# A hybrid decoder layer on one core: the squares of the first norm summed by TensorE, rotary angles moved ahead, the condition row built on chip, and low halves of weights moved from GpSimd to VectorE

## The chip, the core and the metric

The kernel runs on one core of a Trainium2 chip. The core has a matrix engine (TensorE, PE in the profile; its weight loads are PEld), a vector engine (VectorE, DVE), an activation engine (ScalarE, ACT), a general engine (GpSimd, POOL), and a queue engine (SyncE, SP) that issues nearly all transfers. Each engine works through its own queue in order and waits on semaphores. The metric is the device time of one execution in microseconds, as the median of several runs.

## What is computed

One layer (2048 tokens, width 1024): an adaptive norm, one input projection whose columns feed a sliding-window attention and a state-space mixer, an output projection with a gated residual, then the same norm with other weights, a gated feed-forward part of width 2816, another residual and a last norm. What matters for the change:

```python
def rmsnorm(x, w):
    y = x * lax.rsqrt(jnp.mean(x * x, axis=-1, keepdims=True) + EPS)
    return y * w
...
mod = jax.nn.silu(c) @ w_ada[layer] + b_ada[layer]         # c has one row of 1024, mod 6 x 1024
shift1, scale1, gate1, shift2, scale2, gate2 = jnp.split(mod, N_MOD, axis=-1)
h = modulate(rmsnorm(x, norm1_w[layer]), shift1, scale1)   # h * (1 + scale) + shift
x = x + gate1 * hybrid_mixer(h, positions, ...)            # proj = h @ w_in; q and k get rotary angles
```

The rotary step multiplies halves of q and k by the cosine and sine of position times a frequency.

## The kernel before, in words

All matrices are fp32. A large product is made of three products of halves: an operand is split into a high half (a rounded copy, made by ScalarE) and a low half (the rest, made by a subtraction), and `mm3` (L269 to 272) adds high-high, high-low and low-high. So each weight tile costs a load into `raw`, a high half (L262) and a low half (L263) in `weight` (L254 to 267). Before the change L263 runs on GpSimd by default, on VectorE where the caller says so: the first halves of the convolution's weights (L468) and the later output projections (L811). Weights that come again are written back split, and loaded so by the later blocks.

The 2048 tokens are four blocks of 512. Activations lie with the width on the partitions: eight tiles `xT[b, d]` of 128 x 512 for a block. For each block the kernel normalizes x (`norm1`), projects queries, keys and values, convolved channels and gates, then runs attention and the mixer as side work, then the output projection.

`norm1` (L340 to 352) has four steps. It loads the eight tiles, squares them on ScalarE and adds the squares up on GpSimd (`square_into`, L274 to 280); it sums over the partitions with small PE products against ones and takes the reciprocal root by integer tricks on VectorE (`rstd`, L282 to 286, `root_of`, `rsqrt`); it spreads the root over the partitions with four diagonals and one PE product (`spread`, L309 to 315); then it loads x again and makes the modulated halves (`modulated`, L317 to 323). Its later steps are tied to counts of PE's main steps.

The modulation `mod` has 48 columns of 128 values. Column i is a row-wise reduction on VectorE of a tile of `wada` times the silu of c, which lies in `csil` as one row of 1024 on all partitions; before the change `csil` is loaded spread, 512 KB, and its silu taken on the chip (L145 to 151). Four of the first columns come by PE products instead (`ada_products`, L169). The other 32 columns, not needed by the first norm, are made by `ada_later` (L184 to 196): two loads of 256 KB into a ring of two buffers `aw` and two reductions at L195. Their loads are queued behind the opening's last weight load, their reductions behind the opening's last VectorE instruction, by `tc.issue_after`, which puts what is traced in its block, on the named instruction's own engine, behind that instruction in issue order.

Order: in `opening` (L1241) the order of PE, VectorE, SP and ScalarE is written out by hand; it loads x and the first modulation rows, squares, norms, modulates, and runs the first projection as pairs of weight tiles arrive (`pair_ready`, `first_columns`). Its last step is the first quarter of the rotary tables (`rope_tables`, L209 to 231). After it only PE's order is written by hand; the other engines' order comes from a scheduler that works with modelled times and takes what was traced first among what is ready, and it may pull work traced later into gaps of the opening. Rotary steps read cosine and sine at L372 and 373 and are finished at L375, by GpSimd for most blocks. `out_proj` (L805) squares its results for the second norm.

Of the kernel before, what the change touches and what calls it, by code (L numbers as in the profile page):

```python
# [43 lines left out]
def hymba_layer(ctx, tc, xT, crow, pos, wada, wadk, vecs, rows, wq, wkv, wz, wx, wo, wgu, wd, outT):  # L44
# [62 lines left out]
    row = const([P, 32], "row")  # L107
    nc.sync.dma_start(row, rows.broadcast_to([P, 32]))
    posi = const([P, S // P], "posi", I32, pool=ip)
    nc.sync.dma_start(posi, pos)  # L110

# [8 lines left out]
    nc.gpsimd.memset(ones, 1.0)  # L120
    upper = const([P, P], "upper")
# [17 lines left out]
    invf = const([P, HALF], "invf", pool=ip)  # L139
    freqs = np.float32(ROPE_THETA) ** (-np.arange(HALF, dtype=np.float32) / np.float32(HALF))  # L140
    for j in range(HALF):
        nc.gpsimd.memset(invf[:, j:j + 1], float(freqs[j]))
# [3 lines left out]
    nc.sync.dma_start(csil, crow.broadcast_to([P, D]))  # L146

    def silu_c(i):
        cs, th = csil[:, i * T:(i + 1) * T], common.m2()
        nc.scalar.activation(th, cs, AF.Tanh, scale=0.5)  # L150
        nc.vector.scalar_tensor_tensor(cs, th, 1.0, cs, ALU.add, ALU.mult)
# [32 lines left out]
    def ada_later(i):  # L184
        halves = [slice(0, T), slice(T, D)]
        ws = [big("aw", 2, pool=ip) for _ in halves]
        with tc.issue_after(last_fetched.ins):
            for w, hs in zip(ws, halves):
                nc.sync.dma_start(w, wada[i, :, hs])
        for _ in range(2):  # L190
            yield
        m, pt = mod[:, i:i + 1], small([P, 1], "part", 2, pool=ip)
        with tc.issue_after(first_done.ins):
            for w, hs, src, dst in zip(ws, halves, (b_ada[:, i:i + 1], pt), (pt, m)):
                nc.vector.tensor_tensor_reduce(w, w, csil[:, hs], 0.5, src, ALU.mult, ALU.add, dst)  # L195
        yield
# [12 lines left out]
    def rope_tables(lo, hi):  # L209
# [10 lines left out]
        for dst, turn in ((sin, 0.0), (cos, 0.25)):  # L220
            k, r = work(), work()
            nc.vector.tensor_scalar(k, ang, 1.0 / (2 * math.pi), turn, ALU.mult, ALU.add)
            nc.vector.tensor_scalar(k, k, ROUND, None, ALU.add)
            nc.vector.tensor_scalar(k, k, ROUND, turn, ALU.subtract, ALU.subtract)
            nc.vector.scalar_tensor_tensor(r, k, -TWO_PI_1, ang, ALU.mult, ALU.add)
            nc.vector.scalar_tensor_tensor(r, k, -TWO_PI_2, r, ALU.mult, ALU.add)
            nc.vector.scalar_tensor_tensor(r, k, -TWO_PI_3, r, ALU.mult, ALU.add)
            rope_tables.last = nc.vector.tensor_scalar(r, r, PI_IN, -PI_IN, ALU.min, ALU.max)
            angles.append((dst, r))
        for dst, r in angles:  # L230
            nc.scalar.activation(dst[:, lo:hi, :].rearrange("p t j -> p (t j)"), r, AF.Sin)
# [22 lines left out]
    def weight(src, n, key, store, eng=nc.gpsimd, fresh=False):  # L254
# [8 lines left out]
        eng.tensor_tensor(lo, raw[:, :n], hi.bitcast(F32), ALU.subtract)  # L263
# [24 lines left out]
    def root_of(st, n, eng=nc.vector):  # L288
        ms = small([P, NT], "ms", 1, pool=cst)[:, 0:n]
        nc.vector.tensor_scalar(ms, st[:, 0:2 * n].rearrange("p (t k) -> p t k", k=2)[:, :, 0], 1.0 / D, EPS,  # L290
                                ALU.mult, ALU.add)
# [170 lines left out]
    def convolved(b, h):  # L462
        for c in range(8):
            ps = dense()
            for half in range(2):
                if half:
                    yield
                whi, wlo = weight(wx[c, half], T, ("x", c, half), b == 0, nc.gpsimd if half else nc.vector)  # L468
# [336 lines left out]
    def out_proj(b, y_of, mix, bank_of, acc, norm=None, each=lambda c: None):  # L805
        for c in range(KT):
            ps = bank_of(c)
            for half in range(2):
                if half:
                    yield  # L810
                whi, wlo = weight(wo[c, half], T, ("o", c, half), b == 0, nc.gpsimd if b < 2 else nc.vector, b > 1)  # L811
# [8 lines left out]
            square_into(acc, x, c == 0)  # L820
# [420 lines left out]
    def opening():  # L1241
        acc, h, x0 = tmp(), [], []
# [35 lines left out]
        def pair_ready(kp, raws):  # L1278
# [17 lines left out]
            nc.gpsimd.tensor_tensor(ws[2][1], raws[2], ws[2][0].bitcast(F32), ALU.subtract)  # L1296
            first_ws.append(ws)

        rows0, rows1 = rows_of(0, common.m4), rows_of(1, common.m4)
        raws = [fetched(0)]  # L1300
# [5 lines left out]
        rows4, rows5 = rows_of(4, extra.m4), rows_of(5, extra.m4)  # L1306
        reduced(8, rows0[0])
        st, line = side_bank(1), side_bank(0)
        for t in range(NT):
            nc.tensor.matmul(st[:, 2 * t:2 * t + 2], acc[:, t * P:(t + 1) * P], ones[:, 0:2], start=True, stop=True)  # L1310
        reduced(0, rows0[1])
        scale_of(0)
        bc = spread(root_of(st, NT), bc=side_bank(1))
# [24 lines left out]
        rope_tables(0, NT)  # L1338
        return h, main, fetched.last

    first_ws = []
    with tc.manual_schedule(engines={mybir.EngineType.PE, mybir.EngineType.DVE, mybir.EngineType.SP,
                                     mybir.EngineType.Activation}):
        h, main, last_fetched = opening()
        first_done = rope_tables.last
# [69 lines left out]
    with tc.manual_schedule(engines={mybir.EngineType.PE}):  # L1415
        with tc.issue_after(first_done.ins):
# [5 lines left out]
            pending.append([14, lambda: rope_tables(NT, S // P)])  # L1422
# [184 lines left out]
def _layout(x, c, positions, w_ada, b_ada, norm1_w, w_in, conv_w, conv_b, dt_bias, a_log, d_skip, attn_sinks,  # L1607
# [4 lines left out]
    out["crow"] = a(c.reshape(1, D))  # L1612
# [52 lines left out]
```

## Time and profile before

| | us |
|---|---|
| median of three runs | 2269.98 (2266.66 to 2273.71) |
| the profiled execution | 2267.25 |
| its span, first to last instruction | 2265.4 |
| PE busy | 2166.4 |
| VectorE busy | 1681.7 |
| ScalarE busy | 1008.4 |
| GpSimd busy | 700.2 |

The profile's views are: a page with busy times; busy times of each engine in chosen stretches, with the clock that TensorE's throttle granted (1.00 is full speed), the share of time in which the 16 DMA engines were busy, and GB/s; groups of equal instructions by line (busy time, mean ns of one, idle time before them and who ended it); waits (who waited for whom: total, times, longest); and the instructions in order of time (start, duration, engine, line, operation, what ended the idle time before). The lines L are those of the kernel before. An fp32 product of PE is shown as two instructions. The matmuls overlap: their durations are longer than the distance from one to the next.

### The profile page before, as it was taken

The page shows a single profiled execution, that of the slowest core. Times are in us where ns is not written, and L with a number is a line of the kernel's source. Part 1 is how long each engine was busy: PE and PEld are TensorE (multiplying, and loading weights), DVE is VectorE, ACT ScalarE, POOL GpSimd, SP SyncE. Part 2 cuts the span into 40 slices and gives each one's busy share as a digit, 9 for nine tenths or more (in the row PEclk, how much of TensorE's full clock was granted, in tenths as well). Part 3 has the DMA queues.
Part 4 walks back from the last instruction along what each step waited for, and adds up shares of the span by engine and source line. Part 5 has one row for each costly group of instructions (what it writes and reads, how often), then busy time and mean ns, then how long its engine had stood idle before and what let it go on. Part 6 is the DMA issues. An engine that isn't in the chain of part 4 may idle for free. (4 is left out here: it accounts for less than half of the span.)

```text
span 2265.4 us, 33515 instructions
## 1 busy us (share of the span) xinstructions
PE 2166.4 (96%) x11072; PEld 1801.9 (80%) x11072; DVE 1681.7 (74%) x3147; ACT 1008.4 (45%) x2113; POOL 700.2 (31%) x806
## 2 busy tenths in 40 slices
PE   6888988999999999999999999998999999999998
PEld 5778788888978888888888877777888888788887
DVE  8987976774549887788787768987777775776565
ACT  4564543665345655433344444532333333554342
POOL 2655533545123311144342222222333331110021
PEclk9988999999999999999999999999999999999998
DMA  8898988788879523234335579977333335777553
GB/s 296 293 318 298 319 259 258 252 265 271 291 244 339 198 91 110 94 117 126 94 103 182 190 259 310 328 225 227 125 98 105 98 91 197 270 261 268 171 168 100
DMA packets 289325, 470.45 MB, mean 208 GB/s; under 512 B 27392, under 2 KB 97024, under 8 KB 289152
## 3 DMA queue, kind: packets, MB, share of 16 engines
q1 hardware_dynamic: 288576, 467.80, 62.4%
q8 instruction: 87, 1.43, 0.3%
q14 instruction: 86, 0.70, 0.1%
q10 hardware_dynamic: 576, 0.52, 0.1%
HBM read 335.50 MB, written 132.71 MB: 207 GB/s over the span
## 5 line engine op out<-in xcount | busy, mean ns | idle before, releaser
L1090 PE MATMUL d<-a,w 128*128 128x512 f32 x1716 | 405.6, 396 | 7.0 <-DVE a L1062 3.9
L1090 PEld LDWEIGHTS d<-a,w 128*128 128x128 f32 x1716 | 321.6, 188 | 87.8 <-DVE a L1062 5.7
L951 PE MATMUL d<-b,w 128*128 128x512 f32 x924 | 366.0, 400 | 4.4 <-ACT t L975 4.4
L953 PE MATMUL d<-b,w 128*128 128x512 f32 x924 | 366.8, 398 | 1.9 <-DVE w L843 1.9
L952 PE MATMUL d<-b,w 128*128 128x512 f32 x924 | 367.5, 398 | 0.0
L280 POOL TENSOR_TENSOR acc<-acc,t 128x512 f32<-128x512 f32 x70 | 106.2, 1518 | 404.4 <-ACT t L279 389.8
L951 PEld LDWEIGHTS d<-b,w 128*128 128x128 f32 x924 | 174.5, 189 | 44.6 <-ACT t L975 5.5
L842 ACT ACTIVATE w<-s 128x512 fp32r<-128x512 f32 x176 | 110.8, 632 | 221.5 <-PE d L953 174.3
L953 PEld LDWEIGHTS d<-b,w 128*128 128x128 f32 x924 | 174.5, 189 | 42.5 <-DVE w L843 2.6
L952 PEld LDWEIGHTS d<-b,w 128*128 128x128 f32 x924 | 174.9, 189 | 38.6
L270 PE MATMUL d<-w,hl 128*128 128x256 f32 (+1 forms) x592 | 175.8, 297 | 6.9 <-ACT hl L321 4.5
L272 PE MATMUL d<-w,hl 128*128 128x256 f32 (+1 forms) x592 | 171.4, 289 | 1.8 <-DVE hl L322 1.8
L271 PE MATMUL d<-w,hl 128*128 128x256 f32 (+1 forms) x592 | 171.1, 289 | 0.0
L270 PE MATMUL d<-hl,w 128*128 128x512 f32 x352 | 146.3, 416 | 4.3 <-ACT w L262 2.2
L843 DVE TENSOR_TENSOR w<-s,w 128x512 fp32r<-128x512 f32 x176 | 143.2, 815 | 8.6 <-ACT w L842 7.3
L1086 DVE TENSOR_TENSOR w<-raw,w 128x512 fp32r<-128x512 f32 x156 | 107.2, 696 | 53.6 <-ACT w L1085 53.4
L272 PE MATMUL d<-hl,w 128*128 128x512 f32 x352 | 140.5, 399 | 1.4 <-DVE w L263 0.7
L842 ACT ACTIVATE w<-raw 128x512 fp32r<-128x512 f32 x132 | 82.9, 630 | 130.4 <-PE d L953 59.1
L271 PE MATMUL d<-hl,w 128*128 128x512 f32 x352 | 139.6, 397 | 0.0
L1085 ACT ACTIVATE w<-raw 128x512 fp32r<-128x512 f32 x156 | 90.7, 588 | 102.7 <-PE d L1090 67.5
L1062 DVE TENSOR_TENSOR a<-a 128x512 fp32r<-128x512 f32 x154 | 107.5, 720 | 37.3 <-ACT a L1061 37.0
L1005 POOL TENSOR_TENSOR t<-t 128x512 f32<-128x512 f32 x44 | 75.3, 1712 | 180.5 <-DVE t L1004 124.1
(414 smaller groups left out, 5017.7 us busy)
## 6 DMA issues: line engine op xcount, KB each, us to landing
raw<-in_wgu_dram SPq DMA_DIRECT2D x176, 256.0 KB, 2.9
w<-w_x SPq DMA_DIRECT2D x48, 512.0 KB, 5.1
act_t<-t SPq DMA_DIRECT2D x88, 256.0 KB, 3.3
a<-act_t SPq DMA_DIRECT2D x88, 256.0 KB, 4.8
t<-in_xT_dram SPq DMA_DIRECT2D x80, 256.0 KB, 4.2
act_b<-t SPq DMA_DIRECT2D x66, 256.0 KB, 2.2
a<-act_b SPq DMA_DIRECT2D x66, 256.0 KB, 5.0
aw<-in_wada_dram SPq DMA_DIRECT2D x64, 256.0 KB, 4.5
```

The source lines that it names most:

```text
L270: nc.tensor.matmul(out, ahi, bhi, start=first, stop=False)
L271: nc.tensor.matmul(out, ahi, blo, start=False, stop=False)
L272: mm3.last = nc.tensor.matmul(out, alo, bhi, start=False, stop=last)
L280: eng.tensor_tensor(acc, acc, sq, ALU.add)
L842: nc.scalar.activation(hi, x, AF.Copy)
L843: eng.tensor_tensor(lo, x, hi.bitcast(F32), ALU.subtract)
L951: nc.tensor.matmul(out, ahi, bhi, start=first and k == 0, stop=False, skip_group_check=True)
L952: nc.tensor.matmul(out, ahi, blo, start=False, stop=False, skip_group_check=True)
L953: mm3.last = nc.tensor.matmul(out, alo, bhi, start=False, stop=k == 3, skip_group_check=True)
L1062: nc.vector.tensor_tensor(lo, raw, hi.bitcast(F32), ALU.subtract)
L1086: nc.vector.tensor_tensor(w[1], raw, w[0].bitcast(F32), ALU.subtract)
L1090: mm3.last = nc.tensor.matmul(ps, w[x][:, ws], act[k][y][:, ts], start=new and k == 0 and x + y == 0, stop=k == KP - 1 and x == 1, skip_gr ...
```

## The change

- The condition row: the load of `csil` goes. The silu of c is taken on the eight columns that `vec` holds already, and two PE products of ones with diagonals spread it; ScalarE copies it to `csil`.
- The opening's squares: ScalarE squares as before, into a tile of its own each time, and PE adds up with 32 small products into one bank, in place of VectorE's additions and four products. The root now stands ahead of the second reduction.
- The angles of the first rotary quarter are made ahead of the squares, the Sin activations right behind them; both were the opening's last step. The frequencies' memsets stand earlier in GpSimd's queue; the load of the row of constants stands behind the first four modulation rows.
- `norm1` loads x with the tokens on the partitions (`xtok`, again eight tiles of 256 KB); ScalarE's square adds up along the row (`accum_out`), so the additions on GpSimd and the products of `rstd` go.
- `weight` and the third weight of `pair_ready` make every low half on VectorE. `out_proj` adds squares on VectorE for blocks 0 and 1, on GpSimd for 2 and 3 as before.
- `ada_later` names PE's last traced product in `issue_after` for the loads, and nothing for the reductions.

```diff
-    nc.sync.dma_start(csil, crow.broadcast_to([P, D]))
+    def silu_rows():
+        for i in range(2):
+            dg, bk = tmp(), side_bank(i)
+            for j in range(4):
+                nc.vector.tensor_scalar(dg[:, j * P:(j + 1) * P], ident, ccol[:, 4 * i + j:4 * i + j + 1], 0.0,
+                                        ALU.mult, ALU.add)
+            nc.tensor.matmul(bk, ones, dg, start=True, stop=True)
+            nc.scalar.copy(csil[:, i * T:(i + 1) * T], bk)
...
-        with tc.issue_after(last_fetched.ins):
+        with tc.issue_after(mm3.last.ins):
             for w, hs in zip(ws, halves):
                 nc.sync.dma_start(w, wada[i, :, hs])
...
-        with tc.issue_after(first_done.ins):
-            for w, hs, src, dst in zip(ws, halves, (b_ada[:, i:i + 1], pt), (pt, m)):
-                nc.vector.tensor_tensor_reduce(w, w, csil[:, hs], 0.5, src, ALU.mult, ALU.add, dst)
+        for w, hs, src, dst in zip(ws, halves, (b_ada[:, i:i + 1], pt), (pt, m)):
+            nc.vector.tensor_tensor_reduce(w, w, csil[:, hs], 0.5, src, ALU.mult, ALU.add, dst)
...
-        eng.tensor_tensor(lo, raw[:, :n], hi.bitcast(F32), ALU.subtract)
+        nc.vector.tensor_tensor(lo, raw[:, :n], hi.bitcast(F32), ALU.subtract)
...
     def norm1(b, h):
-        acc = sums()
-        for d in range(KT):
-            square_into(acc, load_x(b, d), d == 0)
-        yield
-        y = rstd(acc)
+        ss = small([P, 2, NT], "ssq", 1, pool=ip)
+        for t in range(NT):
+            for i in range(2):
+                x = tmp()
+                nc.sync.dma_start(x, xtok[b * NT + t, i])
+                nc.scalar.activation(x, x, AF.Square, accum_out=ss[:, i, t:t + 1])
+        yield
+        ms = small([P, NT], "ms", 1, pool=cst)
+        nc.vector.tensor_tensor(ms, ss[:, 0, :], ss[:, 1, :], ALU.add)
+        y = root_of_sum(ms, NT)
...
-            square_into(acc, x, c == 0)
+            square_into(acc, x, c == 0, nc.vector if b < 2 else nc.gpsimd)
...
     def opening():
+        silu_columns()
+        silu_rows()
         nc.vector.tensor_copy(posf, posi)
-        silu_columns()
-        for i in range(2):
-            silu_c(i)
+        angles = rope_angles(0, NT)
+        st = side_bank(2)
         for d in range(KT):
-            square_into(acc, x0[d], d == 0, nc.vector)
+            sq = tmp()
+            nc.scalar.activation(sq, x0[d], AF.Square)
+            for t in range(NT):
+                nc.tensor.matmul(st[:, 2 * t:2 * t + 2], sq[:, t * P:(t + 1) * P], ones[:, 0:2], start=d == 0 and t == 0,
+                                 stop=d == KT - 1 and t == NT - 1, skip_group_check=True)
+        rope_tables(angles)
...
-            nc.gpsimd.tensor_tensor(ws[2][1], raws[2], ws[2][0].bitcast(F32), ALU.subtract)
+            last = nc.vector.tensor_tensor(ws[2][1], raws[2], ws[2][0].bitcast(F32), ALU.subtract)
...
         reduced(8, rows0[0])
-        st, line = side_bank(1), side_bank(0)
-        for t in range(NT):
-            nc.tensor.matmul(st[:, 2 * t:2 * t + 2], acc[:, t * P:(t + 1) * P], ones[:, 0:2], start=True, stop=True)
+        bc = spread(root_of(st, NT), bc=side_bank(1))
         reduced(0, rows0[1])
         scale_of(0)
-        bc = spread(root_of(st, NT), bc=side_bank(1))
```

More of the change, by code (lines that the diff above doesn't have):

```diff
@@ L106, in hymba_layer @@
     nc.sync.dma_start(vec, vecs)
-    row = const([P, 32], "row")
-    nc.sync.dma_start(row, rows.broadcast_to([P, 32]))
     posi = const([P, S // P], "posi", I32, pool=ip)
     nc.sync.dma_start(posi, pos)
+    row = const([P, 32], "row")
     b_ada, n1w, n2w, fw_ = vec[:, 0:48], vec[:, 48:56], vec[:, 56:64], vec[:, 64:72]
@@ L120, in hymba_layer @@
     nc.gpsimd.memset(ones, 1.0)
+    invf = const([P, HALF], "invf", pool=ip)
+    freqs = np.float32(ROPE_THETA) ** (-np.arange(HALF, dtype=np.float32) / np.float32(HALF))
+    for j in range(HALF):
+        nc.gpsimd.memset(invf[:, j:j + 1], float(freqs[j]))
     upper = const([P, P], "upper")
@@ L227, in rope_tables @@
             nc.vector.scalar_tensor_tensor(r, k, -TWO_PI_3, r, ALU.mult, ALU.add)
-            rope_tables.last = nc.vector.tensor_scalar(r, r, PI_IN, -PI_IN, ALU.min, ALU.max)
-            angles.append((dst, r))
+            nc.vector.tensor_scalar(r, r, PI_IN, -PI_IN, ALU.min, ALU.max)
+            angles.append((dst[:, lo:hi, :].rearrange("p t j -> p (t j)"), r))
+        return angles
+    def rope_tables(angles):
         for dst, r in angles:
-            nc.scalar.activation(dst[:, lo:hi, :].rearrange("p t j -> p (t j)"), r, AF.Sin)
+            nc.scalar.activation(dst, r, AF.Sin)
     def rsqrt(y, ms, n, eng=nc.vector, tag="rsq", pool=cst):
@@ L252, in hymba_layer, with weight @@
     split_d = {}
[L254 removed]
+    def weight(src, n, key, store, fresh=False):
         two = wt.tile([P, 2, 528], F32R, name="w", tag="w", bufs=SPLIT)
@@ L467, in convolved @@
                     yield
-                whi, wlo = weight(wx[c, half], T, ("x", c, half), b == 0, nc.gpsimd if half else nc.vector)
+                whi, wlo = weight(wx[c, half], T, ("x", c, half), b == 0)
                 for i in range(4):
@@ L810, in out_proj @@
                     yield
-                whi, wlo = weight(wo[c, half], T, ("o", c, half), b == 0, nc.gpsimd if b < 2 else nc.vector, b > 1)
+                whi, wlo = weight(wo[c, half], T, ("o", c, half), b == 0, b > 1)
                 for i in range(4):
@@ L1241, in opening @@
     def opening():
-        acc, h, x0 = tmp(), [], []
+        h, x0 = [], []
         for d in range(KT):
@@ L1295, in pair_ready @@
                 nc.vector.scalar_tensor_tensor(h[d][1], xs[i], sh1[:, d:d + 1], h[d][0].bitcast(F32), ALU.add, ALU.subtract)
-            nc.gpsimd.tensor_tensor(ws[2][1], raws[2], ws[2][0].bitcast(F32), ALU.subtract)
+            last = nc.vector.tensor_tensor(ws[2][1], raws[2], ws[2][0].bitcast(F32), ALU.subtract)
+            pair_done[0] = last
             first_ws.append(ws)
         rows0, rows1 = rows_of(0, common.m4), rows_of(1, common.m4)
+        nc.sync.dma_start(row, rows.broadcast_to([P, 32]))
         raws = [fetched(0)]
@@ L1344, in hymba_layer @@
         h, main, last_fetched = opening()
-        first_done = rope_tables.last
+        first_done = pair_done[0]
     nc.scalar.activation(neg_a, a_log, AF.Exp)
```

27 lines of the change are left out of this document (10 added, 17 removed).

## The prediction

> **What bounds the kernel now.** I read the page first, then the busy times by stage, then TensorE's waits, then the opening in order of time, and last the groups on VectorE and GpSimd.
>
> ```profile
> PE 2166.4 (96%) x11072; PEld 1801.9 (80%) x11072; DVE 1681.7 (74%) x3147; ACT 1008.4 (45%) x2113; POOL 700.2 (31%) x806
> 0.00:30.00 30.00, 11.36 (x26) 3.58 (x26) 22.12 (x49) 10.68 (x18) 6.20 (x50) 1.00 0.93 346
> 30.00:60.00 30.00, 29.98 (x248) 29.55 (x248) 27.62 (x43) 14.27 (x23) 10.46 (x7) 1.00 0.74 246
> 60.00:130.00 70.00, 58.78 (x282) 46.97 (x282) 68.85 (x177) 40.01 (x90) 38.84 (x42) 0.95 0.89 311
> 130.00:240.00 110.00, 95.56 (x673) 88.68 (x672) 83.82 (x212) 58.07 (x138) 65.61 (x77) 0.89 0.91 309
> 240.00:380.00 140.00, 122.96 (x800) 109.90 (x798) 105.85 (x244) 61.31 (x145) 54.83 (x92) 0.96 0.82 266
> 380.00:800.00 420.00, 409.46 (x2506) 352.33 (x2505) 289.08 (x707) 227.93 (x566) 156.64 (x216) 1.00 0.78 263
> ```
>
> TensorE (PE) is busy 96% of the span, so at most 99 us of idle time can be won. The rows by stage (PE busy first, then weight loads, VectorE, ScalarE, GpSimd, granted clock, DMA share) say where it is: 18.6 us before 30, 11.2 in 60 to 130, 14.4 in 130 to 240, 17.0 in 240 to 380, 10.5 in the 420 us after that. From 800 on the change alters nothing, as the late output projections keep VectorE for the low halves and GpSimd for the squares. So the case is decided in the first 380 us. In 60 to 130 VectorE is busy 68.85 of 70 us: it is the bound there. In 130 to 240 it isn't (83.82 of 110), the DMA share is 0.91, and the granted clock is 0.89: PE waits in pieces long enough to lose its clock.
>
> ```profile
> PE d L270 <- ACT w L262: 2.2, 1, 2.2
> PE d L270 <- DVE s L373: 1.1, 1, 1.1
> PE d L270 <- DVE dt L451: 1.0, 1, 1.0
> PE am L271 <- POOL w L263: 1.0, 1, 1.0
> PE d L272 <- POOL w L263: 0.6, 1, 0.6
> PE d L270 <- ACT hl L321: 4.5, 2, 2.4
> PE am L270 <- ACT hl L321: 3.5, 1, 3.5
> ```
>
> These are PE's waits: five in 60 to 130 that the change touches (5.9 us together), then those for the normalized tiles of block 1 (8.0 us).
>
> **The opening, step by step.**
>
> ```profile
> 2.73 0.21 ACT L155 ACTIVATE t<-vec 128x8 f32<-128x8 f32 x1 [0.65 <-DMA vec<-in_vecs_dram]
> 8.57 4.50 ACT L279 ACTIVATE t<-m 128x512 f32<-128x512 f32 x7
> 14.83 1.84 PE L1310 MATMUL at<-ones,t 128*128 128x2 f32 x8 [14.83 <-DVE t L280]
> 17.09 0.15 DVE L290 TENSOR_SCALAR ms<-at 128x4 f32<-128x4 f32 x1
> 19.45 0.88 DVE L312 TENSOR_SCALAR t<-ident,rstd 128x128 f32<-128x128 f32 x4
> 20.24 1.28 DVE L1267 CUSTOM_DVE_ANT_0 m<-m,csil,vec 128x1024 f32<-128x1024 f32 x1
> 20.47 2.04 PE L314 MATMUL at<-t,ones 128*128 128x512 f32 x2 [3.80 <-DVE t L312]
> 22.45 7.68 PE L171 MATMUL am<-hl,vec 128*1 128x512 f32 x16
> 22.72 1.40 DVE L1288 SCALAR_TENSOR_TENSOR t<-m,scl,at 128x512 f32<-128x512 f32 x2
> 30.07 0.38 PE L270 MATMUL d<-w,hl 128*128 128x256 f32 x1
> L285 PE MATMUL d<-ones,acc 128*128 128x2 f32 x40 | 4.8, 241 | 0.0
> 75.62 0.58 ACT L475 COPY cin<-d 128x512 f32<-128x512 f32 x1 [1.81 <-PE d L272]
> ```
>
> Now the condition row no longer comes by a transfer of 512 KB but from the 8 columns. The tanh stays at 2.73; eight diagonals at 0.88 us for four (L312) are done near 5.1; two full-width fp32 products at 2.04 us each (L314) end near 8.3; each is copied by ScalarE at the price of L475, 0.58 us. So the row is whole near 8.9. The squares, behind those copies in ScalarE's order, then run from about 8.9 to 14.0 (eight at 4.50 us for seven), 0.9 us later than now.
>
> VectorE's seven additions go, and PE sums instead: 8 squares by 4 groups of tokens, 32 products, each two instructions, 64 instructions. This price has two ends in the trace. Right after idleness eight of them took 1.84 us (L1310), 0.23 each; in the flow 40 took 4.8 us (L285), 0.12 each. So 7.7 us warm, 14.7 us cold, both slower than ScalarE delivers (0.64 us a square against 0.96 or 1.84): PE sets the pace from the first square's end at 9.5, and the sums end at 17.2 or 24.2 instead of 16.67. PE has run the two products from about 4.2 on and pauses for only a microsecond, so I choose near the warm end: a quarter at the cold price, 16 by 0.23 and 48 by 0.12, 9.4 us, done near 18.9. The Trainium skill (TensorE: Matmul & The Clock Gate, Part 1) says that a busy window of about 3.4 us lifts the clock and an idle one drops it; the two rows above, 0.23 after idleness and 0.12 in the flow, agree. By the rule the time would be the forecast's, by the first row alone about 5 us more; whether such tiny products count as busy, no run here shows.
>
> From the sums the old chain follows: root and diagonals 17.09 to 20.33, 3.3 us; then, since the root now stands ahead of the second reduction, three reductions of 1.21 us and two small steps, 3.8 us, instead of two. The first L1288 thus starts at 18.9 + 0.2 + 3.3 + 3.8 = 26.2 instead of 22.72. Its block is 5.0 us long now; the next fence says what that loses and gains.
>
> ```profile
> 24.64 0.75 DVE L1295 SCALAR_TENSOR_TENSOR hl<-t,mod,hl 128x512 fp32r<-128x512 f32 x1
> 25.49 1.68 POOL L1296 TENSOR_TENSOR w<-raw,w 128x528 fp32r<-128x528 f32 x1 [20.34 <-ACT w L1292]
> 25.91 1.81 DVE L1295 SCALAR_TENSOR_TENSOR hl<-t,mod,hl 128x512 fp32r<-128x512 f32 x1
> L1296 POOL TENSOR_TENSOR w<-raw,w 128x528 fp32r<-128x528 f32 x4 | 6.7, 1675 | 42.7 <-ACT w L1292 42.7
> L263 POOL TENSOR_TENSOR w<-raw,w 128x512 fp32r<-128x512 f32 x24 | 33.5, 1399 | 28.3 <-ACT w L262 21.0 <-DMA raw<-in_wq_dram 3.6 <-DMA aw<-in_wada_dram 3.4
> L263 POOL TENSOR_TENSOR w<-raw,w 128x528 fp32r<-128x528 f32 x12 | 17.3, 1445 | 15.3 <-ACT w L262 15.3
> L280 POOL TENSOR_TENSOR acc<-acc,t 128x512 f32<-128x512 f32 x14 | 20.6, 1473 | 2.9 <-ACT t L279 2.8
> L263 DVE TENSOR_TENSOR w<-raw,w x40: 673/686/1809, 69.2 to 1346.3; 128x512 fp32r<-128x512 f32 x40
> ```
>
> The same L1295 takes 0.75 us, or 1.81 when GpSimd's L1296 runs beside it: 1.06 us lost. The low half on VectorE costs 0.69 us, the median of L263 there. So the block shrinks to 4.6 us, and the first projection product can start near 30.8; PE's own queue (the spread from 22.4, at most 2.0 us, then L171, at most 7.7) is ready by 32.1 at the latest. The old start was 30.07. I put the opening at +1; the warm end gains 1, the cold one loses 6. The Sin step adds a table load and two short activations on ScalarE behind the squares; they fall into its wait for the first weights, behind the same rows of modulation loads as now, so they cost nothing; without that cover they would hold ScalarE for their own length, which I bound by the squares' 4.50 us. The row of constants moves behind four long loads and is first used near 76 us; the reordered memsets are done before the angles need them: nothing.
>
> **60 to 130.** The tables' arithmetic leaves this place:
>
> ```profile
> 55.04 1.42 DVE L216 TENSOR_TENSOR m<-posf,invf 128x128 f32<-128x128 f32 x1
> 64.32 0.75 DVE L195 CUSTOM_DVE_ANT_0 aw<-aw,csil,vec 128x512 f32<-128x512 f32 x1
> L263 DVE TENSOR_TENSOR w<-raw,w 128x512 fp32r<-128x512 f32 x8 | 9.0, 1125 | 0.0
> ```
>
> From 55.04 to 64.32 VectorE did nothing else, and the rotary steps that free the banks queued behind it: 9.3 us come forward. In the opening it runs in the time that the squares' additions leave, from 5.1 on, with at most 9.3 us until 14.4, before the sums are done: no cost; if the additions' room were not there, it would push the root by its length.
>
> Against it stand the low halves: 24 + 12 + 4 in GpSimd's rows, 40 by 0.69 us, 28 us of new VectorE work over 20 to 240. Each waits for ScalarE's high half, and the convolution's steps, which free PE's banks, queue behind it. What it buys: those 40 and the 14 additions L280 of two norms hold GpSimd 78 us (33.5 + 17.3 + 6.7 + 20.6). Their toll on VectorE lies between nothing and 1.06 us each, 57 us. Nearest is VectorE's own L263 in 40 to 240: a mean of 1125 ns against a median of 686 over the run, 0.44 lost. I take half a microsecond for each of the 54, 27 us. The trade alone is even; with the tables, VectorE is about 9 us ahead near 70 us.
>
> Of PE's five waits, 5.9 us, I expect the two on GpSimd, the two on the rotary steps and the ScalarE one, which stands behind them, to go; new ones on VectorE's low halves take 1 back; and of the clock lost there (0.95 over 70 us, 3.5 us) half goes with them, 1.7. That is 5.9 - 1 + 1.7 = 6.6, taken as -7, between -11.2 (all idleness) and 0.
>
> **130 to 380.** The norm of block 1 no longer needs GpSimd. Its eight loads stay eight of 256 KB, and the accumulator reads fall on ScalarE, busy 58 of 110 us: no cost. But its normalization waits for x loads, for VectorE's L319 and L322, which do not change, and for the order of PE's steps. Of the 8.0 us and the cold clock behind them (0.89 over 110 us, at most 12 us) I take a quarter, -5, with bounds -15 and +6 (VectorE later by the even trade gone wrong). For 240 to 800 I take nothing, within 4: VectorE is at 289 of 420 us, which hides 16 low halves and 14 additions of the first two output projections (30 by 0.69 us, 21). The sums by rows remove 24 of the 40 L285 products: 24 by 0.12, -2.9 us, in full, as PE is dense where two of the three norms stand.
>
> **The later modulation rows.** The new helper call names a TensorE instruction, while the block under it issues only loads on SP's queue; it orders only what is traced on the named instruction's own engine. So nothing is paced, and the old order behind the opening's last fetch is dropped, on VectorE too.
>
> ```profile
> SPq L189 <- DVE mod L195: 19.3, 14, 4.0
> SPq L189 <- DVE part L195: 18.0, 14, 2.7
> 42.65 0.91 SPq L189 DMA_DIRECT2D aw<-in_wada_dram  x2
> ```
>
> The old first rows went out at 42.65, right behind that fetch. Now they can go out earlier, wherever SP waits; two buffers hold them to the pace of the reductions as before. I put this at nothing.
>
> Sum: +1 - 7 - 5 - 2.9 = -13.9 us. The profiled execution took 2267.25 us (span 2265.4), 2.7 under the median of 2269.98; the median becomes about 2256.
>
> **Rivals.** *Given back*: the win near 70 us only brings PE sooner to the transfers (share 0.89 to 0.91 from 60 to 240) and the norm's late steps, so that only the opening and the L285 products count, and 2 of the 7: +1 - 2.9 - 2, about 2266. For it speaks the DMA share, against it that it was mean, not full. *Rows loose in the opening*: each row let in ahead of the weights brings 512 KB, 1.5 us at the opening's 346 GB/s, and can hold SP's queue until its reduction is done, up to 4.0 us; two reductions of 0.75 us stand in a full VectorE. That is 7.0 us a row; with the rest at -13.9, two rows bring it level and three make it slower, 2277. For it speaks that the ring's two slots made SP wait 37.3 us from 60 to 380; against it that VectorE has few gaps there. *The whole toll*: if GpSimd costs VectorE the full 1.06 us, 57 us come free instead of 27, and if PE keeps half of the difference: 2241. For it speaks the pair of L1295 rows, against it the mean of L263. The Trainium skill (SBUF — State Buffer, "SBUF: two separate sides") has such a rule: the port that both engines share is an exclusive lock, and the loser is blocked for the whole instruction; the pair agrees. That the change doesn't do what it says holds for the pacing, as read above, and is in the forecast already.
>
> **How the numbers follow.** Forecast 0.50, given back 0.22, loose rows 0.16, whole toll 0.12. This kernel can be told from no change at about 0.3%, 6.8 us. The forecast's own range, 2242 to 2266, holds mostly times faster than that; given back lies within; loose rows count as slower, a cold opening on top of the second as same. Faster 0.62, same 0.21, slower 0.17. For 8 in 10 the range goes from 2236 to 2276.
>
> **What would show it.** Right: the first L270 product near 30, no stall at L372 near 65, VectorE no longer full from 60 to 130, PE idle there down to 4 us, no L285 group of 24. Wrong: sums that end past 22 us with a late L314; modulation rows among the opening's loads and SP waiting on them; VectorE still full at 130 with its low halves waited for by PE.

## The result and the profile after

The changed kernel took 2254.22 us (median of 4, 2253.31 to 2256.79) against 2269.72 for the kernel before: a ratio of 0.9933, 95% interval 0.9915 to 0.995, or 15.5 us less. The profiled execution took 2253.31 us, its span 2251.6. The forecast was 2256. The total was right; several of the terms behind it were not.

First the same stages as before the change (columns as there: PE busy, weight loads, VectorE, ScalarE, GpSimd, granted clock, DMA share, GB/s), and behind them the page's line of engines (busy us, share of the span, instructions).

```profile
0.00:30.00 30.00, 20.51 (x76) 14.43 (x77) 15.84 (x56) 11.82 (x20) 4.65 (x49) 0.72 0.90 337
30.00:60.00 30.00, 27.94 (x202) 23.48 (x199) 29.96 (x63) 10.54 (x19) 0.00 (x0) 1.00 0.69 224
60.00:130.00 70.00, 63.67 (x332) 53.13 (x333) 65.15 (x194) 45.47 (x108) 13.68 (x23) 0.95 1.00 369
130.00:240.00 110.00, 98.92 (x703) 92.57 (x702) 89.73 (x255) 58.72 (x150) 30.04 (x56) 0.91 0.92 318
240.00:380.00 140.00, 127.23 (x857) 115.72 (x856) 97.86 (x244) 60.85 (x150) 51.62 (x97) 0.95 0.80 254
380.00:800.00 420.00, 407.27 (x2455) 349.26 (x2454) 301.18 (x714) 229.41 (x574) 107.69 (x167) 1.00 0.77 260
```

```profile
PE 2170.6 (96%) x11108; PEld 1809.6 (80%) x11108; DVE 1675.7 (74%) x3219; ACT 1009.3 (45%) x2135; POOL 572.0 (25%) x715
```

GpSimd lost 128 us of work (700.2 to 572.0) and VectorE none worth speaking of (1681.7 to 1675.7), although it took over all low halves. TensorE's idle time fell from 11.2 to 6.3 us in 60 to 130, from 14.4 to 11.1 in 130 to 240 and from 17.0 to 12.8 in 240 to 380, and rose from 10.5 to 12.7 in 380 to 800. In the first 30 us TensorE is busier by 9 us, at a granted clock of 0.72 (ahead of the first change on record this column shows 1.00 whatever the clock was, as a_keep below shows). That isn't progress, as its steps in the opening show (start, time, line, operation, count):

```profile
4.95 2.04 PE L152 MATMUL am<-t,ones 128*128 128x512 f32 x2 [4.95 <-DVE t L150]
9.52 12.30 PE L1267 MATMUL sm<-ones,t 128*128 128x2 f32 x64 [1.21 <-ACT t L1265]
25.16 2.07 PE L320 MATMUL at<-t,ones 128*128 128x512 f32 x2 [3.34 <-DVE t L318]
27.16 7.57 PE L173 MATMUL am<-hl,vec 128*1 128x512 f32 x16
34.66 0.39 PE L274 MATMUL d<-w,hl 128*128 128x256 f32 x1
```

The 64 sum products took 12.30 us, 0.19 each, and ended at 21.8, not at 18.9. The spread (L320) started at 25.16, the modulation products (L173) stand behind it in TensorE's order, and the first main product came at 34.66 us instead of 30.07: 4.6 us late. It is not the same in every execution. The six profiles with these sums unaltered (the changed kernel, a_rows, a_low, a_col, a_gadd and a_gmm) have them at 11.21 to 13.81 us, and the first main product at 34.66 to 37.66.

On VectorE, the first step of the root, and the first step on the normalized tiles (L1305 is the old L1288):

```profile
21.85 0.16 DVE L297 TENSOR_SCALAR ms<-sm 128x4 f32<-128x4 f32 x1 [3.95 <-PE sm L1267]
28.77 1.40 DVE L1305 SCALAR_TENSOR_TENSOR t<-m,scl,at 128x512 f32<-128x512 f32 x2
```

TensorE's waits in 60 to 130 are three now. The two on GpSimd, the one on a rotary step (L373), the one on `dt` (L451, a step of the mixer; the prediction counts it as rotary) and those on high halves (L262) are gone. The longest one before, which the prediction does not list, has changed its cause: the product of L584, now L595, waited for VectorE's reciprocal root and now waits for a load of a stored projection. First the line of the kernel before, then all three of the changed one:

```profile
PE at L584 <- DVE rsq L249: 3.9, 1, 3.9
```

```profile
PE at L595 <- DMA m<-q: 6.0, 1, 6.0
PE d L275 <- DVE w L1311: 0.8, 1, 0.8
PE d L276 <- DVE hl L1312: 0.3, 1, 0.3
```

The later modulation rows do go out earlier, between the opening's weight loads (SP's queue):

```profile
20.80 1.62 SPq L1274 DMA_DIRECT2D raw<-in_wq_dram  x2
23.36 1.61 SPq L191 DMA_DIRECT2D aw<-in_wada_dram  x2
30.81 0.33 SPq L1274 DMA_DIRECT2D raw<-in_wkv_dram  x1
```

### The profile page after: what moved, and what is told of

It reads as the page before. It is cut to its first block, busy times and chain, and to the rows that moved or that the text cites. A ratio compares the mean times of both kernels' runs of the same rounds, so it can differ in the third digit from the quotient of the medians.

```text
span 2251.6 us, 33562 instructions
## 1 busy us (share of the span) xinstructions
PE 2170.6 (96%) x11108; PEld 1809.6 (80%) x11108; DVE 1675.7 (74%) x3219; ACT 1009.3 (45%) x2135; POOL 572.0 (25%) x715
## 5 line engine op out<-in xcount | busy, mean ns | idle before, releaser
L284 POOL TENSOR_TENSOR acc<-acc,t 128x512 f32<-128x512 f32 x35 | 56.4, 1612 | 339.6 <-ACT t L283 311.6
L274 PEld LDWEIGHTS d<-w,hl 128*128 128x128 f32 x592 | 117.1, 198 | 14.1 <-ACT hl L327 5.6
```

The costliest lines, as they stand in the source:

```text
L274: nc.tensor.matmul(out, ahi, bhi, start=first, stop=False)
```

## The experiments

Twelve kernels, each a part done alone on the kernel before or a part undone, or a cost added, on the changed one. Medians in us, with the ratio to the kernel before (2269.27, 2268.91 and 2269.08 in the three groups) and its 95% interval:

| kernel | median | ratio, interval |
|---|---|---|
| changed: squares added by VectorE (a_add) | 2249.49 | 0.992, 0.9907 to 0.9934 |
| changed: rows' order as before (a_rows) | 2251.41 | 0.9924, 0.9911 to 0.9938 |
| changed: both (a_two) | 2249.29 | 0.9912, 0.9898 to 0.9926 |
| changed: both, products ahead of the spread (a_three) | 2250.47 | 0.9914, 0.9901 to 0.9927 |
| changed: one wide product a square more (a_keep) | 2263.60 | 0.9973, 0.9961 to 0.9985 |
| before: low halves on VectorE (b_low) | 2263.02 | 0.9976, 0.9966 to 0.9986 |
| changed: low halves on GpSimd (a_low) | 2259.46 | 0.9959, 0.9946 to 0.9972 |
| before: tables first (b_rope) | 2266.32 | 0.9988, 0.9978 to 0.9998 |
| before: norm by rows (b_xtok) | 2257.98 | 0.9949, 0.9936 to 0.9961 |
| changed: norm by columns (a_col) | 2266.86 | 0.9985, 0.9974 to 0.9995 |
| changed: GpSimd additions put in (a_gadd) | 2265.10 | 0.9984, 0.9972 to 0.9995 |
| changed: two-column products put in (a_gmm) | 2256.54 | 0.994, 0.9927 to 0.9954 |

An interval is about 3 us to each side, so differences of 3 us between two of these rows are open, and those of 5 us are seen only where the runs lie apart. The changed kernel itself was timed in a session of its own (2254.22, against 2269.72 for the kernel before). No run takes the condition row built on chip by itself.

**The opening's sums (a_add).**

```diff
-            sq = tmp()
-            nc.scalar.activation(sq, x0[d], AF.Square)
-            for t in range(NT):
-                nc.tensor.matmul(st[...], sq[...], ones[:, 0:2], ...)
+            square_into(acc, x0[d], d == 0, nc.vector)
+        for t in range(NT):
+            nc.tensor.matmul(st[...], acc[...], ones[:, 0:2], start=True, stop=True)
```

> The changed kernel, but its opening squares are added up by VectorE as before (seven additions and four products with two columns, in place of 64 instructions of TensorE). Theory: the 64 ran at 0.19 us each, the root came at 21.85 us, and with it the spread, the modulation products and the first product of the main stream, at 34.66 us instead of 30.07 in the kernel before; with the additions the root comes near 16.5, the first main product near 30, and the time falls by 3 to 5 us under the changed kernel's 2254.2, to about 2250. Rival (the later waits on transfers take it back): the first product comes 4 us earlier, but the time stays within 1 us of 2254.

Measured 2249.49, 4.7 less than the changed kernel (the ends of the runs overlap: 2248.4 to 2254.1 against 2253.3 to 2256.8). TensorE's steps show what moved:

```profile
15.91 1.87 PE L1266 MATMUL sm<-ones,t 128*128 128x2 f32 x8 [7.22 <-DVE t L284]
21.21 2.04 PE L320 MATMUL at<-t,ones 128*128 128x512 f32 x2 [3.44 <-DVE t L318]
23.19 7.54 PE L173 MATMUL am<-hl,vec 128*1 128x512 f32 x16
30.66 0.39 PE L274 MATMUL d<-w,hl 128*128 128x256 f32 x1
```

The first main product is back at 30.66, 4.0 us earlier. That the gain stays in the end is seen only together with the rows' edit, in a_two further down, whose runs lie apart from the changed kernel's. VectorE had room for both: in the changed kernel the angles took it from 5.76 to 9.97 us, and the additions start at 10.39 here.

**What the sums cost TensorE (a_keep).** In the changed kernel the granted clock (the last column but two) fell to half at about 11 us, and stayed there while TensorE had no gap:

```profile
9.00:12.00 3.00, 2.48 (x19) 2.48 (x19) 0.86 (x4) 3.00 (x7) 0.00 (x0) 0.87 1.05 416
12.00:15.00 3.00, 3.00 (x16) 3.00 (x16) 1.29 (x2) 2.95 (x7) 0.00 (x0) 0.50 0.93 373
15.00:18.00 3.00, 3.00 (x15) 3.00 (x16) 0.17 (x1) 1.43 (x2) 0.00 (x0) 0.50 0.85 312
18.00:21.00 3.00, 3.00 (x15) 3.00 (x16) 0.00 (x0) 1.26 (x2) 0.00 (x0) 0.50 1.04 423
24.00:27.00 3.00, 1.84 (x2) 0.50 (x2) 2.93 (x9) 0.00 (x0) 0.00 (x0) 0.50 1.03 409
27.00:30.00 3.00, 3.00 (x7) 0.55 (x7) 3.00 (x7) 0.45 (x1) 0.00 (x0) 0.79 0.99 382
```

At 9 to 12 us 19 of the products took 2.48 us, 0.13 each; at 15 to 18, 15 took 3.00, 0.20 each. The clock comes back only when the wide products of 25.16 and 27.16 have run for some 3 us. How much they cost depends on the execution, too: where the profile shows 13.81 us for the 64 (a_gadd, a_gmm), all of them ran at 0.22. The column shows 1.00 there, and that is no reading. It is what the column shows until the first change on record. The wide product of 4.95 us took 2.04 us under such a 1.00, as long as the one of 25.16 at 0.50 (2.07); at full clock one takes 1.13 (L321 of a_three, below). So the clock was at half at 4.95 us, and in the kernel before at 20.47 (L314, 2.04 us), though the prediction's row of the first 30 us shows 1.00. For a_keep a wide product was put between the small ones:

```diff
             nc.scalar.activation(sq, x0[d], AF.Square)
+            nc.tensor.matmul(side_bank(3)[:, 0:T // 2], ones, sq[:, 0:T // 2], start=True, stop=True)
             for t in range(NT):
```

> The changed kernel with one extra fp32 product of 256 columns ahead of each square's four two-column products in the opening; its result is used by nothing. In the changed kernel the granted clock fell to half at about 11.5 us although TensorE ran the two-column products without a gap, and the price of each rose from 0.13 to 0.19 us. Theory, tiny products do not count as activity and wide ones do: the clock stays at 1.0 from 9 to 20 us, the small products take 0.12 to 0.13 each, and the sums end at 21 to 22 us in spite of the added work; time 2252 to 2256. Rival, anything sets the clock to half there: 0.5 from 12 us on, the wide products at about 1 us each, and the sums end at 28 to 30 us; time about 2260.

Measured 2263.60, and the clock fell all the same (steps of TensorE, then a stretch of 3 us):

```profile
10.22 0.70 PE L1266 MATMUL st<-t,ones 128*128 128x256 f32 x2 [1.20 <-ACT t L1265]
10.76 0.95 PE L1268 MATMUL sm<-ones,t 128*128 128x2 f32 x8
18.80 1.20 PE L1266 MATMUL st<-t,ones 128*128 128x256 f32 x2
19.79 1.71 PE L1268 MATMUL sm<-ones,t 128*128 128x2 f32 x8
21.36 1.20 PE L1266 MATMUL st<-t,ones 128*128 128x256 f32 x2
27.47 1.71 PE L1268 MATMUL sm<-ones,t 128*128 128x2 f32 x8
```

```profile
18.00:21.00 3.00, 3.00 (x14) 2.82 (x13) 0.00 (x0) 0.39 (x1) 0.00 (x0) 0.50 1.02 418
```

The theory as I put it fell: the clock didn't stay, and the sums ended at 29.2. But the rival's "anything" isn't shown either. From 18.80 to 19.79 TensorE is in the wide product and from there to the next wide one at 21.36 in the eight small ones: wide work in 0.99 of 2.56 us wasn't enough to bring the clock back; wide work alone was. What the bound between them is stays open. The rival's figures are nearer for all that (2263.6 against about 2260, the sums' end at 29.2 against 28 to 30). The same eight products cost 0.95 us at full clock and 1.71 at half.

**Half of the modulation products earlier (a_three).** This edit stands on those of a_add and a_rows.

```diff
-        bc = spread(root_of(st, NT), bc=side_bank(1))
+        y = root_of(st, NT)
+        ada_products(first, line, range(4))
+        bc = spread(y, bc=side_bank(1))
...
-        ada_products(first, line, range(8))
+        ada_products(first, line, range(4, 8))
```

> The same two parts undone, and half of the opening's modulation products ahead of the spread of the root on TensorE, in the 3.4 us in which it waits for the root. Theory: the first product of the main stream stood right behind these products at 30.66 us, so it comes about 2 us earlier, and the time falls by 1 to 2 us under that with two parts. Rival: their rows have not landed by then, the spread stands behind them, and the time rises by up to 4 us. Rival two: VectorE's last low half of the first pair, at 29.2 us, is the next to be waited for, and the gain is under 1 us.

2250.47 against the 2249.29 of a_two, on which this edit stands: nothing gained. Their rows landed late:

```profile
20.47 5.12 PE L173 MATMUL am<-hl,vec 128*1 128x512 f32 x8 [2.70 <-DMA hl<-in_wadk_dram]
25.52 1.13 PE L321 MATMUL at<-t,ones 128*128 128x512 f32 x2
30.10 0.39 PE L275 MATMUL d<-w,hl 128*128 128x256 f32 x1
```

Against a_two's profile the spread moved from 21.52 to 25.52, and the first main product came 1.4 us earlier (30.10 for 31.46), without a gain in time. What the first rival says of the rows and of the spread came true; a rise isn't seen beyond the noise.

**The rows' order (a_rows, a_two).** a_two has this edit and that of a_add.

```diff
-        with tc.issue_after(mm3.last.ins):
+        with tc.issue_after(last_fetched.ins):
...
+        with tc.issue_after(first_done.ins):
             for w, hs, src, dst in ...:
```

> The changed kernel, but the later modulation rows' loads stay behind the opening's last weight load on SP's queue, and their reductions behind the opening's last step on VectorE, as before. Theory (the row that got into the opening fills a gap of VectorE and of the queue): the time stays within 2 us of 2254.2. Rival one, loose rows: each row let in costs up to 7 us, two got in before 42 us, so the time falls by 5 us or more, to 2249 or less. Rival two, the early rows are a gain, as the last of them is loaded at 314 us instead of 345: the time rises by 2 to 5 us.

> The changed kernel with two parts undone together: the opening's squares added by VectorE, and the later modulation rows behind the opening's last weight load. Theory: each alone took 4.7 and 2.8 us from 2254.2 and they touch different places, so the time is about 2247. Rival, both bring TensorE sooner to the same wait for the stored projections near 100 us: 2249 to 2250.

a_rows took 2251.41, 2.8 under the changed kernel, within what an interval leaves open; on top of a_add the same edit is worth 0.2 us (2249.49 to 2249.29). So a row let in costs far less in the end than the 7.0 us of the rival. That the two gains add up is not borne out (2249.29 against 2247), but the difference is within the noise. a_two's runs (2247.6 to 2250.7) lie wholly under the changed kernel's (2253.3 to 2256.8); from a_add and a_three it can't be told apart.

**Low halves (b_low, a_low).** b_low:

```diff
-        eng.tensor_tensor(lo, raw[:, :n], hi.bitcast(F32), ALU.subtract)
+        nc.vector.tensor_tensor(lo, raw[:, :n], hi.bitcast(F32), ALU.subtract)
...
-            square_into(acc, x, c == 0)
+            square_into(acc, x, c == 0, nc.vector if b < 2 else nc.gpsimd)
```

> The kernel before with one part alone: all low halves of weights on VectorE, and the additions of the second norm's squares in the first two blocks too, none of it on GpSimd. Theory, the even trade: 28 us of new VectorE work stand against 27 us of toll taken away, so the time stays within 4 us of 2269.7. Rival, the whole toll: VectorE loses less than it gains, TensorE keeps half of the difference, the time falls by 10 us or more. Rival, pure cost: VectorE, full from 60 to 130 us, is late by up to 20 us there, and the time rises by 5 us or more.

> The changed kernel with this part undone: the low halves and the second norm's additions of the first two blocks back on GpSimd. Theory, the parts add up: alone on the kernel before this was worth 6 us, so 2254.2 becomes about 2260. Rival, the parts overlap, since the tables and the row norm have already given VectorE its room in 60 to 130: under 3 us. Rival two, without that room the toll weighs more: over 9 us.

Done alone 6.2 us less, undone 5.2 us more. In the kernel before, VectorE made 8 low halves from 30 to 240 us, in 9.0 us (the row of L263 in the prediction). In b_low:

```profile
L263 DVE TENSOR_TENSOR w<-raw,w 128x512 fp32r<-128x512 f32 x32 | 23.4, 733 | 8.2 <-ACT w L262 8.1
L263 DVE TENSOR_TENSOR w<-raw,w 128x528 fp32r<-128x528 f32 x12 | 11.6, 986 | 0.0
```

and the stages of b_low in that time:

```profile
30.00:60.00 30.00, 29.63 (x248) 29.25 (x246) 26.97 (x53) 16.80 (x28) 3.96 (x3) 1.00 0.71 244
60.00:130.00 70.00, 62.12 (x329) 51.74 (x330) 66.31 (x190) 44.46 (x94) 20.81 (x29) 0.98 0.94 342
130.00:240.00 110.00, 92.57 (x632) 86.25 (x631) 89.90 (x240) 55.30 (x137) 39.83 (x59) 0.88 0.91 311
```

There are 36 more of them, 26.0 us, and yet VectorE's busy time in that stretch rose by 2.9 us only (27.62 + 68.85 + 83.82 = 180.29, and 26.97 + 66.31 + 89.90 = 183.18 in b_low). In busy time the trade is even to 3 us. In 60 to 130 TensorE gains: it is busy 62.12 of 70 us instead of 58.78, at a clock of 0.98, and no wait on GpSimd is left there; a half takes 0.73 us (0.99 with 528 columns) and not GpSimd's 1.40 (1.45). But this lead does not last. Of 130 to 240 TensorE is busy 92.57 us instead of 95.56, and counted along the instructions of `mm3`, the one with 500 ahead of it starts at 128.1 us instead of 141.3, the one with 1000 ahead at 234.3 instead of 235.4. So for this part alone the rival of the prediction, given back, held up to 235 us, and where the 6.2 us of the end come from stays open.

**Tables (b_rope).**

```diff
         silu_columns()
+        nc.vector.tensor_copy(posf, posi)
+        angles = rope_angles(0, NT)
...
             square_into(acc, x0[d], d == 0, nc.vector)
+        rope_tables(angles)
...
-        rope_tables(0, NT)
         return h, main, fetched.last
```

> The kernel before with one part alone: the rotary angles worked out in the opening, the two Sin steps behind the squares, nothing of it at 55 us. Theory: the 9.3 us of VectorE near 55 us come forward, the waits of TensorE on the rotary steps near 70 us go, and the time falls by 4 to 7 us, to about 2264. Rival, given back: the transfers and the norm of block 1 set the pace behind, and the time stays within 2 us of 2269.7.

2.9 us less (interval 0.5 to 5.0), between theory and rival. TensorE gained 2.2 us of busy time in 60 to 130, but lost 3.9 in 130 to 240, where the clock was 0.85 in this run (240 to 380 gave 6.2 back):

```profile
60.00:130.00 70.00, 60.94 (x304) 49.89 (x302) 64.29 (x168) 42.56 (x92) 43.73 (x46) 0.95 0.94 338
130.00:240.00 110.00, 91.61 (x639) 85.94 (x640) 87.81 (x212) 55.20 (x133) 63.73 (x71) 0.85 0.87 296
```

The 9.3 us were not all the tables' own. The same step, first in the kernel before and then in the opening of the changed one, where GpSimd is idle by then:

```profile
56.50 1.24 DVE L222 TENSOR_SCALAR m<-m 128x128 f32<-128x128 f32 x1
```

```profile
6.07 0.23 DVE L223 TENSOR_SCALAR m<-m 128x128 f32<-128x128 f32 x1
```

All the arithmetic takes 4.2 us there (5.76 to 9.97). At 55 us the first five steps took 6.4 us instead of 1.3, beside five steps of GpSimd: a toll of 1.0 us for each of these. In b_rope such tolls can fall on other steps, as GpSimd keeps its work; and the angles, ahead of the squares' additions, move the sums from 14.83 to 16.00 us and the first main product from 30.07 to 32.22. That this is why the theory's 4 to 7 us didn't come is argued, not tested.

**The norm along rows (b_xtok, a_col).** b_xtok is the diff's norm1 and root_of_sum on the kernel before; a_col is the reverse on the changed kernel.

> The kernel before with one part alone: the first norm of blocks 1 to 3 sums along rows on ScalarE, so that 12 of the two-column products and 21 additions of GpSimd go. Theory, the products alone: 24 instructions by 0.12 us, 2.9 us less, and a little of the stretch that GpSimd puts on VectorE near 60 us; 2269.3 becomes about 2266. Rival, the norm comes ready earlier and TensorE's waits for block 1's normalized tiles go with it (8.0 us before): 2261 or less. Rival, the loads of whole rows are no better than those of columns and the products stand in gaps: within 1.5 us of 2269.3.

> The changed kernel with this part undone: the first norm of blocks 1 to 3 adds its squares on GpSimd and sums them by two-column products, as in the kernel before. Theory: the same 2.9 us and as much again for the additions' stretch on VectorE, 21 by about 0.6 us where VectorE is near full, a third of them: 2254 becomes 2257 to 2261. Rival, products alone: 2257. Rival, it is worth nothing: within 1.5 us of 2254.

10.9 us less alone, 12.6 us more when undone: the largest part of the change by far, and both times beyond the theory. The time is that of the first rival of b_xtok, but not for its reason: TensorE's waits for block 1's normalized tiles are still there in b_xtok (5.8 us on L323, where 8.0 stood). Two kernels take its two halves apart.

**The additions alone and the products alone (a_gadd, a_gmm).** What they add is used by nothing.

```diff
                 nc.scalar.activation(x, x, AF.Square, accum_out=ss[:, i, t:t + 1])
+                if k:
+                    nc.gpsimd.tensor_tensor(acc, x if k == 1 else acc, x, ALU.add)
+                k += 1
```

```diff
+        st = norm_bank()
+        for t in range(NT):
+            nc.tensor.matmul(st[:, 2 * t:2 * t + 2], x[:, t * P:(t + 1) * P], ones[:, 0:2], start=True, stop=True)
         y = root_of_sum(ms, NT)
+        nc.vector.tensor_scalar(ss[:, 1, :], st[...], 1.0 / D, EPS, ALU.mult, ALU.add)
```

> The changed kernel, with seven additions of 128x512 on GpSimd put back into each of the three row norms; their result is used by nothing, and the norm doesn't wait for them. This prices GpSimd's company alone. Theory now: undoing the row norm cost 12.6 us, of which the two-column products are 2.9; the additions stretched VectorE's steps by about 0.6 us each where it is full (5.9 us in 60 to 80 us against 0.4 in the changed kernel), so 21 of them raise 2254.2 by 5 to 9 us. Rival one: the stretch lies in VectorE's slack, under 2 us; then the norm's own chain is what cost. Rival two, even less: nothing.

> The changed kernel, with four two-column products put back into each of the three row norms (24 instructions in all), in a bank of the main stream, read by one short step of VectorE behind the root; nothing uses the result. Theory: TensorE is dense there, so they cost 24 by 0.12, 2.9 us, and 2254.2 becomes 2257. Rival one: they wait for the last square and hold TensorE's order as in the kernel before, 5 us or more. Rival two: they stand in idle time, under 1 us.

The 21 additions cost 10.9 us though in the trace nobody waits for them, 0.52 us each; the 24 instructions 2.3 us, near 24 by 0.12, but within the noise. Together 13.2, near a_col's 12.6. The stretch from 60 to 80 us, where the first seven fall, with VectorE's low halves of 528 columns in it; the changed kernel:

```profile
60.00:80.00 20.00, 19.67 (x134) 18.02 (x135) 17.26 (x54) 11.33 (x29) 0.00 (x0) 1.00 0.91 325
```

```profile
L267 DVE TENSOR_TENSOR w<-raw,w 128x528 fp32r<-128x528 f32 x4 | 2.7, 708 | 2.0 <-ACT w L266 2.0
```

and with the additions:

```profile
60.00:80.00 20.00, 17.98 (x114) 16.89 (x115) 19.84 (x42) 12.55 (x30) 10.52 (x7) 0.83 0.75 265
```

```profile
L267 DVE TENSOR_TENSOR w<-raw,w 128x528 fp32r<-128x528 f32 x4 | 5.9, 1505 | 0.2 <-ACT w L266 0.2
```

Seven steps of GpSimd make VectorE full (19.84 of 20 us), and the low halves that they meet take 1505 ns for 708. TensorE's busy time and clock in this row (17.98 and 0.83 instead of 19.67 and 1.00) are not the additions' doing, for a_gmm has them without any:

```profile
60.00:80.00 20.00, 17.91 (x118) 16.97 (x117) 16.79 (x51) 13.07 (x30) 0.00 (x0) 0.83 0.81 288
```

In both executions the opening had run late (first main product at 37.08 and 37.66 us), so a_gmm's trace is the one to compare a_gadd's with. From the first of these low halves to the first step on `dt` VectorE takes 14.57 us with the additions and 12.39 without, and its idle time of 3.2 us in between shrinks to 0.2: 5.2 us of stretching for seven steps. TensorE pays nothing for it there: counted along `mm3`, the instruction with 400 ahead of it starts at 105.3 us, in a_gmm at 105.6. It pays at the second and the third norm, at 239.3 instead of 235.6 (1000 ahead) and at 422.2 instead of 412.9 (1800 ahead). At the third a short step of the norm's own root shows why, first without the additions and then with them, and behind it the wait of TensorE that follows:

```profile
404.08 0.16 DVE L252 TENSOR_TENSOR rsq<-rstd 128x4 f32<-128x4 f32 x1
```

```profile
407.87 1.14 DVE L252 TENSOR_TENSOR rsq<-rstd 128x4 f32<-128x4 f32 x1
```

```profile
PE am L274 <- DVE m L675: 2.8, 1, 2.8
```

Four steps of the root that take about 0.16 us without the additions take 1.1 each with them. From the root's first step (L297) to L675 VectorE needs 6.1 us instead of 2.3. A product of the attention waits for L675, and the clock falls behind the wait (400 to 420 us: TensorE busy 16.23 us at 0.84, instead of 19.30 at 1.00). So here a step of GpSimd was paid for where TensorE needed VectorE next, and a chain of short steps paid most.

These are single executions, and a_gadd's profiled one is among its slowest (2271.48 us, median 2265.10); it loses some 7 us more between 690 and 920 us, where it has no additions. And a_gadd isn't the old norm: there the root waits for the additions and can't run beside them. a_col loses its time at other places (8 us by the 500th instruction), so the agreement of the totals doesn't show that the additions act in both alike.

By the Trainium skill (SBUF — State Buffer, "SBUF: two separate sides") a VectorE step with two SBUF inputs waits out the GpSimd step that holds the shared port. The traces agree that such steps are held (1505 ns for 708). What it cost the kernel here is 0.52 us for each GpSimd step of 1.1 to 1.7 us, not the whole of it.

## Why the prediction came out right, and which terms were wrong

- **Opening, +1: mis-sized.** It was 4.6 at the first main product, and undoing the sums gave 4.7 back. The step that failed is "I choose near the warm end: a quarter at the cold price": the 64 instructions took 0.19 us each, as the clock was at half for most of them, and in two other executions 0.22, the cold price nearly in full. Its second half failed too, "ready by 32.1 at the latest": that bound started from the chosen end of the sums, 18.9, and is no bound. With the sums' end at 21.8 its own terms give 35.0, and 34.66 was measured. The loss stayed within the stated 6 us here, but is 7.0 and 7.6 in the profiles of a_gadd and a_gmm. Of the signs, sums past 22 us with a late L314 came nearly (21.8 and 25.16); the first product near 30 did not come. The condition row (squares from 8.83 us, 8.9 was forecast) and the Sin steps, done at 14.9 and ahead of a wait for weights, were right.
- **60 to 130, -7: more in the end, by other parts.** Idle time fell by 4.9, not to the 4 us that were to show it; the clock gave nothing (0.95 both times). Counted along TensorE's `mm3` instructions it is more: 4.6 us behind at the first, 7.3 ahead at the one with 500 ahead of it (134.0 us for 141.3), 11.9 together in these two executions. The waits that were listed went, as foreseen, but a load of 6.0 us stands where an unlisted wait of 3.9 stood. And the cause that I gave most to, the tables, is worth 2.9 us alone: of their 9.3 us only 4.2 were their own.
- **"The trade alone is even": true of VectorE's busy time, wrong as a term of the time.** 26.0 us of low halves for 2.9 us of busy time, but 6.2 us less alone. That every half on VectorE is ready in about half of GpSimd's time was not counted; whether that is what makes the 6.2, no run shows.
- **The norm: mis-sized by far.** Its -2.9 for the products fits (2.3, within the noise). The failing step is that I counted 14 of the norm's 21 additions among the 54 steps that pay for the low halves, and so booked their gain at nothing. No VectorE work takes the place of the norm's additions, as ScalarE sums along with its squares: all 21 tolls, 10.9 us, are gain. That this is 0.52 us a step, and half a microsecond was put, is chance: the one is the kernel's time, the other VectorE's. VectorE's was 0.75 (5.2 for seven steps in a_gadd), 1.0 (beside the tables) and 0.64 (23.1 us for the 36 halves of b_low).
- **130 to 380, -5: right in sign.** Idle time fell by 7.6 us, and counted along `mm3` the lead grew by 3.6, to 10.9 at 383 us; the norm's additions at 200 to 220 us are part of it.
- **Rows, 0: right within 3 us.** The pacing orders nothing, and rows went out at 23.36, as read from the code. Of the loose rows' price of 7.0 us each nothing was to be seen in the end.

The parts measured by themselves add up: 4.7 us lost in the opening and 0.2 to 2.8 with the rows; 10.9, 6.2 and 2.9 won with the norm, the low halves and the tables. That is 12.5 to 15.1 us less, against 15.5, and each part has some 3 us of noise. That my sum came so near is in part luck: a loss of 3.6 us more in the opening and the tables' 4 us too much were made up by the 8 us of the norm and the 6 of the low halves that I hadn't booked, or only as part of the 5 in 130 to 380. "Given back" didn't happen as a whole, though it did for the low halves alone up to 235 us; "the whole toll" had the right cause, and on VectorE a size between its 1.06 us a step and the half. That the price of the sums rises with the half clock is shown within one trace (0.13 to 0.20 us each; 0.95 to 1.71 us for eight in a_keep); why two-column products leave the clock at half isn't settled.

## What to carry to other kernels

Where VectorE is full, a GpSimd step that nobody waits for isn't free: book its toll (here half a microsecond of the kernel's time for a step of about 1.4), and look first for work on GpSimd that can vanish altogether, such as sums that ScalarE's accumulator makes on the way. The length of a VectorE step in a profile can hold such a toll already: compare it with the same step where GpSimd is idle before you book it as work. When a step is moved to TensorE ahead of everything, price it at the cold clock (0.22 us here, not 0.12) and follow what stands behind it in TensorE's own order. And compare two traces stage by stage only when both came into the stage alike. And when several edits are summed, don't let the gain of one pay for the cost of another in the same line: write each edit's term by itself.

## What the hardware showed that I had not expected

TensorE was busy without a gap from 12 to 21 us with products of two columns, at a granted clock of 0.50, and a wide product of 256 columns in 39% of the time (0.99 of 2.56 us) didn't raise it; a stream of wide products alone brought it back in about 3 us. The Trainium skill (TensorE: Matmul & The Clock Gate, Part 1) says that a busy window of about 3.4 us lifts the clock; here busy in the profile's sense wasn't enough.
